# A transformer block on one core: seven-product pairs in the feed-forward stage, its operand normed first, the p product moved

## The chip, the cores and the metric

The kernel runs on one core of a Trainium2 chip. The metric is the device time of one execution in microseconds (us). The kernel before took 1504.08 us, the median of three runs from 1503.74 to 1504.20 us. The profile is one further execution, which took 1504.06 us. Its recorded span, from the first instruction to the last, is 1502.4 us, so 1.7 us lie around the span.

## The reference, cut to what matters

```
x: 256 tokens x 2048 (fp32); p: 256 x 256; w_in: 2048 x 10240; w_ffn_in: 2048 x 11264; w_ffn_out: 5632 x 2048
h   = rmsnorm(x, g_mix);  q, k, v (two mixers of 8 heads) and two gates = h @ w_in
x  += (sigmoid(g_sb) * (y_sb @ w_sb_out) + sigmoid(g_ca) * (y_ca @ w_ca_out)) @ w_mix_out     # "mix"
h   = rmsnorm(x, g_ffn);  g_ff, u_ff = split(h @ w_ffn_in, 2)
x  += (silu(g_ff) * u_ff) @ w_ffn_out                                                         # "FFN"
x  += sigmoid(rmsnorm(x, g_ple) @ w_ple_gate) * (p @ w_ple_in)                                # gate, p product
out = rmsnorm(x, g_final)
```

All data are fp32. The 256 tokens are two tiles of 128 (`t` = 0, 1); the 2048 columns of x are sixteen k tiles of 128 (`kt`).

## The kernel before, in words

**Products.** A product of fp32 matrices is made from rounded parts. Each operand is split into `hi` (rounded to the type fp32r) and `lo` (the rest, rounded too), and three TensorE matmuls are summed in PSUM: hi·hi, hi·lo, lo·hi (`row_products`, L178 to L183). The activations are the stationary operand: tables `T1`, `T2`, `T3` hold x, h or the like transposed, as 16 k tiles x (hi, lo) x 256 tokens. The weights move, 512 columns at a time.

**Pieces.** A group is one block of 512 weight columns for both token tiles. `group` (L126) cuts it into pieces of two k tiles (128x1024 numbers, 512 KB). A piece is loaded by SP into one of five `raw` buffers (L144), split by ScalarE (`hi`, L173) and VectorE (`lo`, L174) into one of three `hi` and three `lo` buffers, and used by 12 matmuls (2 k tiles x 2 token tiles x 3). `flush` (L223) writes the pieces out in order; `prefetch` (L208) keeps the loads five pieces and the splits two pieces ahead. After each piece one entry of the list `tasks` is written out, and `later` (L217) puts three empty entries ahead of its own. When a split needs a part of a table that isn't written, tasks are run until it is.

**Order on the engines.** The text order is only a priority: when the program is built, a scheduler sets the order of instructions on each engine by its own estimate of when each is ready. On the chip each engine keeps its order, and waits are semaphores.

**Tables.** `into_table` (L242) transposes four 128-column blocks of both token tiles on TensorE into PSUM (8 transposes), ScalarE copies or scales them to `hi` (L250, L256) and VectorE makes `lo` (L251, L257).

**Stages.** (1) Start: x is transposed into T1, the first v group runs, then the p product (`w_ple_in`, 4 groups of one piece, stored to memory by `pin_post`). (2) The rest of `w_in` with both attentions. (3) The out projections and the mix product; `residual_post` (L600) adds each mix block to x, sums its squares, and three pieces later puts the un-normed x into T3 with the gain `g_ffn`. (4) FFN in three blocks of 16, 16 and 12 k tiles of the hidden dimension: for each 512 hidden columns a gate group and an up group of `w_ffn_in` (8 pieces each); `g_post` and `u_post` (L630, L640) apply the token factor `rstd_ffn` and the SwiGLU, and the result goes into T2 or T1. Then four groups of `w_ffn_out` add to x. (5) The `w_ple_gate` groups and the output.

Of the kernel before, what the change touches and what calls it, by code (L numbers as in the profile page):

```python
# [35 lines left out]
LOAD_AHEAD = 5  # L36
SPLIT_AHEAD = 2
# [3 lines left out]
def block_kernel(ctx: ExitStack, tc: tile.TileContext, x, p, w_in, w_sb_out, w_ca_out, w_mix_out,  # L41
                 rel_bias, g_mix, g_ffn, g_ple, g_final, w_ffn_in, w_ffn_out, w_ple_in, w_ple_gate,
                 out):

# [20 lines left out]
    def aux(name):  # L65
        return ps_ax[-1][0].tile([P, ps_ax[-1][1]], F32, tag="ax", name=name)
# [7 lines left out]
    const("fill", [P, 832])  # L74
# [20 lines left out]
    def square_sum(n, t, c, pool):  # L95

        jk = pool.tile([P, NB], F32, tag="jk", name="jk", bufs=1)
        nc.scalar.activation(jk, x_[:, t, c * NB : (c + 1) * NB], AF.Square, accum_out=sums[n][:, t, c : c + 1])  # L98
# [27 lines left out]
    def group(kind, wsrc, n0, kts, lhs, post, needs=lambda kt: None, row0=0, keep=None):  # L126
# [4 lines left out]
        for j in range(0, len(kts), nk):  # L131
            part = kts[j : j + nk]
            r = (row0 + j) * P
            pieces.append(dict(
                g=g, kts=part, ncol=ncol, first=j == 0, last=j + nk >= len(kts),
                src=wsrc[r : r + len(part) * P, n0 : n0 + ncol].rearrange("(k p) n -> p k n", p=P),
                needs=[k for k in (needs(kt) for kt in part) if k is not None],
            ))

# [3 lines left out]

    def load(pc):  # L144
        raw = wp.tile([P, 1024], F32, tag="raw", name="raw", bufs=5)
        pc["raw"] = raw
        n = len(pc["kts"]) * pc["ncol"]
        dst = raw[:, :n].rearrange("p (k n) -> p k n", n=pc["ncol"])
        at = state["loaded"]
        if at == 0:  # L150
            for k in range(2):
                if k:
                    load_x(k, 1)
                dma_w.dma_start(dst[:, k, :], pc["src"][:, k, :])
            return
        if at < KD // 2:
            load_x(2 * at, 2)
        dma_w.dma_start(dst, pc["src"])

    def split(pc):  # L160
# [11 lines left out]
        for c in range(0, n, m):  # L172
            nc.scalar.copy(hi[:, c : c + m], raw[:, c : c + m])  # L173
            nc.vector.tensor_tensor(lo[:, c : c + m], raw[:, c : c + m], hi.bitcast(F32)[:, c : c + m], ALU.subtract)  # L174
# [3 lines left out]
    def row_products(ps, lhs, kt, t, hi, lo, a, z):  # L178
        xh = lhs[:, kt, 0, t * P : (t + 1) * P]
        xl = lhs[:, kt, 1, t * P : (t + 1) * P]  # L180
# [3 lines left out]

    def products(pc):
        g = pc["g"]
        if pc["first"]:
            g["ps"] = [ps_mm.tile([P, 512], F32, tag="mm", name=f"mm{t}") for t in range(2)]
# [12 lines left out]
        del pc["hi"], pc["lo"]  # L201
# [4 lines left out]
    state = dict(loaded=0, split=0, at=0)  # L206
# [35 lines left out]
    def into_table(dst, c, src, gain=None, key=None):  # L242

        ps = aux("tp").rearrange("p (k s) -> p k s", k=4)
        for k in range(4):
            for t in range(NT):
                nc.tensor.transpose(ps[:, k, t * P : (t + 1) * P], src[:, t, k * P : (k + 1) * P], ident)  # L247
        ks = slice(4 * c, 4 * c + 4)
        if gain is None:
            nc.scalar.copy(dst[:, ks, 0, :], ps)  # L250
            nc.vector.tensor_tensor(dst[:, ks, 1, :], ps, dst.bitcast(F32)[:, ks, 0, :], ALU.subtract)  # L251
        else:
            for k in range(4):
# [20 lines left out]
    pT = sp.tile([P, 2, 2, S], F32R, tag="pT", name="pT")  # L274
# [52 lines left out]
    tasks.append(("p", p_transposes))  # L327
# [13 lines left out]
    def pin_post(c):  # L341
        def post(ps):
            if c == 0:
                while "v" not in done:
                    run_task()
            st = sp.tile([P, NT, NB], F32, tag="pst", name="pst", bufs=2)
            for t in range(NT):
                nc.scalar.copy(st[:, t, :], ps[t])
            dma_x.dma_start(pin_d[:, :, c * NB : (c + 1) * NB], st)
        return post  # L350
# [11 lines left out]
    ps_ax.append((ctx.enter_context(tc.tile_pool(name="ps_ax", bufs=2, space=PSUM)), 1024))  # L362


    att = ExitStack()
    ap = att.enter_context(tc.tile_pool(name="att", bufs=2))
# [231 lines left out]
    late = {}  # L598

    def residual_post(c, key, gain):  # L600

        def post(ps):
# [3 lines left out]
            if key is not None:  # L606
                for t in range(NT):
                    square_sum(key, t, c, late["pool"])
                if c == 3:
                    norm(key)  # L610
                dst = T1 if key == "ple" else late["T3"]
                later(lambda: into_table(dst, c, x_[:, :, cs], gain, key))
        return post

    for c in range(4):
        group("row", w_mix_out[0], c * NB, range(KD), T1, residual_post(c, "ffn", 16), needs=lambda kt: ("mg", kt))
# [7 lines left out]
    gf = lp.tile([P, D], F32, tag="gf", name="gf")  # L624
    dma_x.dma_start(gf, g_final.rearrange("(o d) -> o d", o=1).to_broadcast((P, D)))
    flush()

    hold = {}

    def g_post(j):  # L630
        def post(ps):
            sg = lp.tile([P, NT, NB], F32, tag="sg", name="sg")
            tg = hold[j] = lp.tile([P, NT, NB], F32, tag="tg", name="tg")
# [136 lines left out]
```

## Time and profile before

| | |
|---|---|
| median of three runs | 1504.08 us |
| profiled execution | 1504.06 us |
| its span | 1502.4 us |
| TensorE matmuls busy | 1488.2 us (99%) |
| VectorE busy | 851.3 us (57%) |
| ScalarE busy | 700.8 us (47%) |
| DMA, mean over the span | 192 GB/s |

Busy time is the sum of what an engine's records cover; share is of the span. Records of neighbouring matmuls overlap, so the time that a matmul costs is read from start to start, not from its duration. A line such as L174 is the line of the kernel that issued the instruction. Idle time of an engine is put down to what it waited for.

### The profile page before, as it was taken

To read this page: it belongs to the slowest core of one execution; us is meant where nothing else is said; L and a number is where in the kernel's file an instruction comes from. 1 tells how busy PE (TensorE), PEld (TensorE's weight loads), DVE (VectorE), ACT (ScalarE), POOL (GpSimd) and SP (SyncE) were. 2 spreads that over 40 slices of the span, in tenths; PEclk is the share of its full clock that TensorE was granted. 3 is DMA by queue.
4 is the path that set the end of the run, shared out by engine and by line. 5 is a ranking of instruction groups with operands and counts; after the bars stand their busy time and mean duration, and the time that the engine had idled before them with its cause. 6 is when DMAs were issued, how large, how long until landed. Compare 5 with 4: busy or idle time off the path is not lost.

```text
span 1502.4 us, 18130 instructions
## 1 busy us (share of the span) xinstructions
PE 1488.2 (99%) x7024; PEld 1243.8 (83%) x7024; DVE 851.3 (57%) x936; ACT 700.8 (47%) x831; POOL 24.1 (2%) x45
## 2 busy tenths in 40 slices
PE   8999999999999999999999999999999999999997
PEld 6888888888888888888888888888888888888886
DVE  6566666665444565555554555455455455556576
ACT  6555554556444434554444433444443344445443
POOL 1200000000000000000000000000000000000000
PEclk9999999999999999999999999999999999999999
DMA  7865555565666666666666666666666666666573
GB/s 270 299 202 169 173 177 177 180 177 174 191 196 192 188 182 220 185 185 193 184 185 193 194 186 195 195 185 193 184 193 191 191 195 189 203 204 184 183 222 119
DMA packets 164807, 289.06 MB, mean 192 GB/s; under 512 B 9040, under 2 KB 44160, under 8 KB 164464
## 3 DMA queue, kind: packets, MB, share of 16 engines
q1 hardware_dynamic: 162560, 278.96, 61.4%
q0 software_dynamic: 2160, 8.93, 1.8%
q8 instruction: 55, 0.90, 0.2%
q14 instruction: 32, 0.26, 0.1%
HBM read 282.09 MB, written 5.77 MB: 192 GB/s over the span
## 4 chain that ended last, share of the span: by engine, by line
PE 98%; issue 1%; DMA 0%; DVE 0%; SPq 0%; POOL 0%; POOLq 0%; ACT 0%; DVEq 0%
PE mm L183 28%; PE mm L181 28%; PE mm L182 28%; PE mm L198 8%; PE mm L200 4%; PE tp L247 1%; DMA x<-in_x 0%; PE xps L286 0%; PE yp L443 0%; PE wt L534 0%; PE zp L434 0%; PE zp L433 0%; PE zp L432 0%; PE yp L434 0%; PE yp L432 0%
## 5 line engine op out<-in xcount | busy, mean ns | idle before, releaser
L174 DVE TENSOR_TENSOR lo<-raw,hi 128x1024 fp32r<-128x1024 f32 (+1 forms) x517 | 632.4, 1224 | 593.3 <-ACT hi L173 592.3
L173 ACT CAST hi<-raw 128x1024 fp32r<-128x1024 f32 (+1 forms) x517 | 543.1, 1051 | 685.3 <-PE mm L183 592.5
L182 PE MATMUL mm<-lo,T 128*128 128x512 f32 x1792 | 700.4, 391 | 0.0
L183 PE MATMUL mm<-hi,T 128*128 128x512 f32 x1792 | 697.6, 390 | 0.0
L181 PE MATMUL mm<-hi,T 128*128 128x512 f32 x1792 | 640.2, 392 | 0.0
L183 PEld LDWEIGHTS mm<-hi,T 128*128 128x128 f32 x1792 | 336.7, 188 | 69.4
L182 PEld LDWEIGHTS mm<-lo,T 128*128 128x128 f32 x1792 | 337.0, 188 | 68.6
L181 PEld LDWEIGHTS mm<-hi,T 128*128 128x128 f32 x1792 | 336.7, 188 | 68.8
L198 PE MATMUL mm<-T,hi 128*128 128x512 f32 x512 | 180.3, 398 | 0.0
L200 PE MATMUL mm<-T,lo 128*128 128x256 f32 x512 | 140.8, 280 | 0.0
L198 PEld LDWEIGHTS mm<-T,hi 128*128 128x128 f32 x512 | 95.3, 188 | 21.5
L200 PEld LDWEIGHTS mm<-T,lo 128*128 128x128 f32 x512 | 96.3, 189 | 1.2
L237 ACT COPY tm<-mm 128x256 f32<-128x256 f32 x32 | 11.9, 373 | 24.2 <-PE mm L200 24.2
L605 DVE TENSOR_TENSOR x<-mm,x 128x512 f32<-128x512 f32 x32 | 20.5, 682 | 0.0
L636 ACT ACTIVATE sg<-mm,rstd_ffn 128x512 f32<-128x512 f32 x22 | 15.0, 690 | 10.9 <-PE mm L183 10.9
L256 ACT ACTIVATE T<-tp,gT 128x256 fp32r<-128x256 f32 x32 | 15.0, 468 | 10.5 <-DVE T L257 10.5
L239 DVE TENSOR_TENSOR sm<-mm,tm 128x256 f32<-128x256 f32 x32 | 13.5, 421 | 10.4 <-ACT tm L237 10.4
L637 DVE SCALAR_TENSOR_TENSOR tg<-mm,rstd_ffn,sg 128x512 f32<-128x512 f32 x22 | 15.7, 751 | 5.0 <-ACT sg L636 5.0
L251 DVE TENSOR_TENSOR T<-tp,T 128x1024 fp32r<-128x1024 f32 x15 | 18.3, 1220 | 0.3
L257 DVE SCALAR_TENSOR_TENSOR T<-tp,gT,T 128x256 fp32r<-128x256 f32 x32 | 15.4, 480 | 4.3 <-ACT T L256 4.3
L98 ACT ACTIVATE jk<-x 128x512 f32<-128x512 f32 x24 | 15.1, 628 | 2.1 <-DMA x<-in_x 1.7
L250 ACT CAST T<-tp 128x1024 fp32r<-128x1024 f32 x15 | 15.2, 1013 | 1.1 <-PE tp L247 1.1
(166 smaller groups left out, 537.5 us busy)
## 6 DMA issues: line engine op xcount, KB each, us to landing
raw<-in_w_ffn_in SPq DMA_DIRECT2D x176, 512.0 KB, 3.7
raw<-in_w_in SPq DMA_DIRECT2D x159, 512.0 KB, 3.6
raw<-in_w_ffn_out SPq DMA_DIRECT2D x88, 512.0 KB, 4.6
raw<-in_w_mix_out SPq DMA_DIRECT2D x32, 512.0 KB, 4.0
raw<-in_w_ple_gate SPq DMA_DIRECT2D x32, 512.0 KB, 4.4
raw<-in_w_sb_out SPq DMA_DIRECT2D x16, 512.0 KB, 4.6
raw<-in_w_ca_out SPq DMA_DIRECT2D x16, 512.0 KB, 4.5
raw<-in_w_ple_in SPq DMA_DIRECT2D x4, 512.0 KB, 4.9
```

What stands on the lines that cost most here:

```text
L173: nc.scalar.copy(hi[:, c : c + m], raw[:, c : c + m])
L174: nc.vector.tensor_tensor(lo[:, c : c + m], raw[:, c : c + m], hi.bitcast(F32)[:, c : c + m], ALU.subtract)
L181: nc.tensor.matmul(ps, xh, hi, start=a, stop=False)
L182: nc.tensor.matmul(ps, xh, lo, start=False, stop=False)
L183: nc.tensor.matmul(ps, xl, hi, start=False, stop=z)
L198: nc.tensor.matmul(ps, hi[:, i, f], lhs[:, kt, :, :].rearrange("p c s -> p (c s)"), start=a, stop=False)
L200: nc.tensor.matmul(ps[:, :S], lo[:, i, f], lhs[:, kt, 0, :], start=False, stop=z)
L250: nc.scalar.copy(dst[:, ks, 0, :], ps)
L251: nc.vector.tensor_tensor(dst[:, ks, 1, :], ps, dst.bitcast(F32)[:, ks, 0, :], ALU.subtract)
L257: nc.vector.scalar_tensor_tensor(dst[:, kt, 1, :], ps[:, k, :], g, dst.bitcast(F32)[:, kt, 0, :], ALU.mult, ALU.subtract)
L605: nc.vector.tensor_tensor(x_[:, t, cs], ps[t], x_[:, t, cs], ALU.add)
L637: nc.vector.scalar_tensor_tensor(tg[:, t, :], ps[t], r, sg[:, t, :], ALU.mult, ALU.mult)
```

## The change

FFN products are no longer made group by group but in units of two column groups: for the first product the gate block and the up block of the same 512 hidden columns, for the second product two neighbouring blocks of 512 output columns. There are 11 units of the first kind and 6 of the second. A unit has 8 pairs of k tiles (6 in the second product of the last block). Pairs 2 and 4 are made by a form of Strassen's scheme with seven products instead of eight; the operands' 2x2 blocks are two token tiles by two k tiles, and two k tiles by two column groups. Each of the seven is made from three matmuls of 512 columns as before.

For such a pair the weights need three sums more (t2, t3, t4, made by VectorE and split like the others into `xh` and `xl`, which lie in a free table), and the activations need four sums (`forms`, made in `into_table`, kept in `F_in` and `F_out`). Four of the seven products go to PSUM banks of their own (`sums`), which `mid` adds up in SBUF (`C`) after pair 4; the unit's ends add `C` to the ordinary sums. PSUM is now two pools of four banks that alternate between the units.

T3 now holds the normed operand: after the last mix block, when `rstd_ffn` is known, `normal_table` scales x by it and writes the table, four tasks in all. The p product no longer runs at the start but after the mix, behind the same tasks. From the mix on there is a fourth pair of hi and lo buffers (`buffers`), and the splits may run further ahead (`prefetch`). Other edits only share buffers anew.

```diff
+PAIRS = (2, 4)
+RAW = 5
+    def unit(wsrc, n0s, kts, lhs, forms, ext, mid, post, needs, row0=0):
+        state["unit"] = state.get("unit", -1) + 1
+        pool, side = late["ps"][:: 1 if state["unit"] % 2 == 0 else -1]
...
+            if i in PAIRS:
+                pieces.append(dict(pc, src=src, pair=True, first=i == PAIRS[0], last=i == PAIRS[-1]))
+            else:
+                for b in range(2):
+                    pieces.append(dict(pc, src=[src[b]], block=b, first=i == 0, last=2 * i + 2 == len(kts)))
...
+    def split_pair(pc, raw1, raw2):
...
+        xl, xh = room[:, :1536], room[:, 1536:]
+        xf = late["pool"].tile([P, 1536], F32, tag="xf", name="xf")
...
+        (h1, l1), (h2, l2) = buffers(1024), buffers(1024)
+        nc.scalar.copy(h1, raw1)
+        minus(t3, b[1][:, 1, :], b[1][:, 0, :])
+        minus(b[1][:, 0, :], b[1][:, 0, :], b[0][:, 0, :])
+        nc.scalar.copy(h2, raw2)
+        minus(t2, b[1][:, 1, :], b[1][:, 0, :])
+        minus(t4, b[0][:, 1, :], t2)
+        nc.scalar.copy(xh, xf)
+        minus(l1, raw1, h1.bitcast(F32))
+        minus(l2, raw2, h2.bitcast(F32))
+        minus(xl, xf, xh.bitcast(F32))
...
+    def pair_products(pc):
...
+        if a:
+            while tasks:
+                run_task()
+            g["sums"] = [g["side"].tile([P, 512], F32, tag="mm", name=f"su{i}") for i in range(4)]
...
+        for ps, x, w, own in ((q1, (kt, 0), 0, True), (c11, (kt2, 0), 1, False), (c12, 3, 3, False), (q5, 0, 2, True),
+                              (q6, 1, 4, True), (q7, 2, 5, True), (c21, (kt2, 1), 6, False)):
+            three(ps, *stationary(x), hi[w], lo[w], a and own, z and own)
+        if z:
+            g["mid"](g)
...
     def prefetch():
-        while state["loaded"] < min(len(pieces), state["at"] + LOAD_AHEAD + 1):
+        while state["loaded"] < len(pieces) and state["raw"] + len(pieces[state["loaded"]]["src"]) <= RAW:
...
-        ahead = 1 if state["at"] < KD // 2 else SPLIT_AHEAD
-        while state["split"] < min(len(pieces), state["at"] + ahead + 1):
-            split(pieces[state["split"]])
+        room = 2 if state["at"] < KD // 2 else 4 if "pool" in late else 3
+        while state["split"] < state["loaded"] and state["split"] <= state["at"] + 3:
+            pc = pieces[state["split"]]
+            if state["split"] > state["at"] and sum(map(size, pieces[state["at"] : state["split"] + 1])) > room:
+                break
+            split(pc)
...
+    def into_table(dst, c, src, gain=None, key=None, forms=None, pool=None):
...
+            if forms is not None and kt // 2 in PAIRS:
+                af = late["pool"].tile([P, 2, S], F32, tag="af", name="af", bufs=2)
...
+                nc.vector.tensor_tensor(fm[:, 0, :], a21, a22, ALU.add)
+                minus(fm[:, 2, :], a11, a21)
+                minus(fm[:, 1, :], fm[:, 0, :], a11)
+                minus(fm[:, 3, :], a12, fm[:, 1, :])
+                f = forms(kt)
+                nc.scalar.copy(f[:, 0], fm)
+                minus(f[:, 1], fm, f.bitcast(F32)[:, 0])
...
+    def normal_table(c):
+        xn = late["pool"].tile([P, NT, NB], F32, tag="sg", name="xn")
+        for t in range(NT):
+            nc.scalar.activation(xn[:, t, :], x_[:, t, c * NB : (c + 1) * NB], AF.Identity,
+                                 scale=rstd["ffn"][:, t : t + 1])
+        into_table(late["T3"], c, xn, 16, "ffn", lambda kt: late["F"][0][kt // 4 - 1])
+    def mix_post(c):
...
+            residual_done(c, "ffn")
+            if c == 3:
+                for cc in range(4):
+                    tasks.append((None, lambda cc=cc: normal_table(cc)))
...
-    for c in range(4):
-        group("row", w_ple_in[0], c * NB, range(2), pT, pin_post(c), needs=lambda kt: "p")
...
+    tasks.append(("p", p_transposes))
+    for c in range(4):
+        group("row", w_ple_in[0], c * NB, range(2), pT, pin_post(c), needs=lambda kt: "p")
+    flush()
...
+    def mid(g):
+        q1, q5, q6, q7 = g["sums"]
+        C = g["C"] = lp.tile([P, 4, NB], F32, tag="C", name="C", bufs=2)
+        nc.scalar.copy(C[:, 0, :], q1)
+        for i, q, j in ((2, q6, 0), (1, q7, 2), (3, q5, 1), (2, q5, 2)):
+            nc.vector.tensor_tensor(C[:, i, :], q, C[:, j, :], ALU.add)
+    def in_post(dst, c, key):
+        def post(g, b):
+            C = g["C"]
+            for t in range(NT):
+                i = 2 * b + t
+                nc.vector.tensor_tensor(C[:, i, :], g["ps"][i], C[:, i, :], ALU.add)
+            if b == 0:
+                sg = lp.tile([P, NT, NB], F32, tag="sg", name="sg")
+                for t in range(NT):
+                    nc.scalar.activation(sg[:, t, :], C[:, t, :], AF.Sigmoid)
+                for t in range(NT):
+                    nc.vector.tensor_tensor(C[:, t, :], C[:, t, :], sg[:, t, :], ALU.mult)
+            else:
+                for t in range(NT):
+                    nc.vector.tensor_tensor(C[:, t, :], C[:, t, :], C[:, 2 + t, :], ALU.mult)
+                later(lambda: into_table(dst, c, C[:, :2, :], key=key, pool=g["pool"],
+                                         forms=lambda kt: late["F"][1][kt // 4 - 1]))
...
+        for c in (0, 2):
+            unit(w_ffn_out[0], (c * NB, (c + 1) * NB), range(nk), T2, lambda kt: late["F"][1][kt // 4 - 1],
+                 T3 if last else T1, mid, out_unit_post(c, last), lambda kt, key=key: (key, kt), row0=k0)
```

`out_unit_post` adds the PSUM block to `C` and `C` to x (two VectorE instructions for each token tile); in the last block it also sums squares and puts x into T1 for the gate.

## Rows read from the trace of the kernel before

**Rows 1.** Page: busy us, share of the span, instructions, by engine.

```profile
PE 1488.2 (99%) x7024; PEld 1243.8 (83%) x7024; DVE 851.3 (57%) x936; ACT 700.8 (47%) x831; POOL 24.1 (2%) x45
```

**Rows 2.** Page: the chain that ended last, share by engine.

```profile
PE 98%; issue 1%; DMA 0%; DVE 0%; SPq 0%; POOL 0%; POOLq 0%; ACT 0%; DVEq 0%
```

**Rows 3.** Stretches: us, busy by engine (instructions), granted clock, DMA share, GB/s.

```profile
0.00:60.00 60.00, 54.71 (x261) 44.70 (x262) 34.89 (x53) 36.45 (x59) 9.57 (x21) 1.00 0.81 273
...
671.40:1404.30 732.90, 732.90 (x3290) 606.72 (x3289) 387.17 (x361) 313.72 (x329) 2.23 (x3) 1.00 0.64 191
```

**Rows 4.** Timeline of TensorE, mix stage: start us, us, instruction; starts of pieces, transposes.

```profile
649.10 0.62 PE L181 MATMUL mm<-hi,T 128*128 128x512 f32 x2
...
651.82 0.62 PE L181 MATMUL mm<-hi,T 128*128 128x512 f32 x2
...
654.54 0.62 PE L181 MATMUL mm<-hi,T 128*128 128x512 f32 x2
655.00 0.60 PE L247 MATMUL tp<-ident,x 128*128 128x128 f32 x4
...
657.75 0.60 PE L247 MATMUL tp<-ident,x 128*128 128x128 f32 x4
```

**Rows 5.** Groups by shape: count, busy us, mean ns, idle before it.

```profile
L174 DVE TENSOR_TENSOR lo<-raw,hi 128x1024 fp32r<-128x1024 f32 x515 | 631.0, 1226 | 592.5 <-ACT hi L173 591.4
L173 ACT CAST hi<-raw 128x1024 fp32r<-128x1024 f32 x515 | 541.9, 1053 | 684.6 <-PE mm L183 592.5 <-PE mm L198 52.6 <-issue 29.8
...
L605 DVE TENSOR_TENSOR x<-mm,x 128x512 f32<-128x512 f32 x32 | 20.5, 682 | 0.0
```

**Rows 6.** Timeline of VectorE: a dense stretch of attention, then the tail.

```profile
264.25 1.23 DVE L174 TENSOR_TENSOR lo<-raw,hi 128x1024 fp32r<-128x1024 f32 x1 [2.57 <-ACT hi L173]
265.39 0.42 DVE L427 TENSOR_TENSOR sl<-qT,sh 128x256 fp32r<-128x256 f32 x1
265.73 0.69 DVE L427 TENSOR_TENSOR sl<-kT,sh 128x512 fp32r<-128x512 f32 x1
266.33 0.69 DVE L410 TENSOR_TENSOR T<-yp,T 128x512 fp32r<-128x512 f32 x1
...
1482.82 0.69 DVE L683 TENSOR_TENSOR sgr<-sgr,pi 128x512 f32<-128x512 f32 x1 [1.51 <-ACT sgr L682]
1483.54 0.69 DVE L684 TENSOR_TENSOR x<-x,sgr 128x512 f32<-128x512 f32 x1
```

**Rows 7.** Timeline of ScalarE and VectorE: one split, waiting for a free buffer.

```profile
601.08 1.05 ACT L173 CAST hi<-raw 128x1024 fp32r<-128x1024 f32 x1 [1.67 <-PE mm L183]
602.17 1.23 DVE L174 TENSOR_TENSOR lo<-raw,hi 128x1024 fp32r<-128x1024 f32 x1 [1.49 <-ACT hi L173]
```

**Rows 8.** Timeline of three engines: last mix block to the norm.

```profile
671.59 1.28 DVE L605 TENSOR_TENSOR x<-mm,x 128x512 f32<-128x512 f32 x2
674.71 0.17 DVE L104 TENSOR_SCALAR ms_ffn<-ms_ffn 128x2 f32<-128x2 f32 x1
674.96 0.73 POOL L105 TENSOR_TENSOR rstd_ffn<-ms_ffn,mhalf 128x2 f32<-128x2 f32 x1 [85.89 <-DVE ms_ffn L104]
```

**Rows 9.** Timeline of ScalarE: small table steps, and stores of the p product.

```profile
681.65 0.47 ACT L256 ACTIVATE T<-tp,gT 128x256 fp32r<-128x256 f32 x1
...
48.01 1.08 ACT L348 COPY pst<-mm 128x512 f32<-128x512 f32 x2 [2.40 <-DMA pin_d<-pst]
```

**Rows 10.** Timeline of TensorE: first matmuls after the idle start, then later ones.

```profile
7.83 0.63 PE L183 MATMUL mm<-hi,T 128*128 128x512 f32 x1
8.26 0.63 PE L182 MATMUL mm<-lo,T 128*128 128x512 f32 x1
...
11.99 0.40 PE L182 MATMUL mm<-lo,T 128*128 128x512 f32 x1
12.22 0.39 PE L183 MATMUL mm<-hi,T 128*128 128x512 f32 x1
```

**Rows 11.** Page, DMA issues: queue, count, KB each, us to landing.

```profile
raw<-in_w_ffn_in SPq DMA_DIRECT2D x176, 512.0 KB, 3.7
```

More of the change, by code (lines that the diff above doesn't have):

```diff
@@ L95, in square_sum @@
     def square_sum(n, t, c, pool):
[L97 removed]
+        jk = pool.tile([P, NB], F32, name="jk", **(dict(tag="af", bufs=2) if pool is late.get("pool") else dict(tag="jk", bufs=1)))
         nc.scalar.activation(jk, x_[:, t, c * NB : (c + 1) * NB], AF.Square, accum_out=sums[n][:, t, c : c + 1])
@@ L142, in load_x, with load_piece, buffers, minus @@
         dma_w.dma_start(x_[:, :, cs], xr[:, :, cs])
+    def load_piece(src, ncol):
+        raw = wp.tile([P, 1024], F32, tag="raw", name="raw", bufs=RAW)
+        n = src.shape[1] * ncol
+        return raw[:, :n], raw[:, :n].rearrange("p (k n) -> p k n", n=ncol)
     def load(pc):
[L145 to L148, printed above, removed]
         at = state["loaded"]
[L150 to L158, printed above, removed]
+        pc["raw"] = []
+        for src in pc["src"]:
+            raw, dst = load_piece(src, pc["ncol"])
+            pc["raw"].append(raw)
+            state["raw"] += 1
+            if at == 0:
+                for k in range(2):
+                    if k:
+                        load_x(k, 1)
+                    dma_w.dma_start(dst[:, k, :], src[:, k, :])
+                continue
+            if at < KD // 2:
+                load_x(2 * at, 2)
+            dma_w.dma_start(dst, src)
+    def buffers(n):
+        state["hl"] += 1
+        i = state["hl"]
+        out = []
+        for tag in ("hi", "lo"):
+            if "pool" in late and i % 4 == 0:
+                t = late["pool"].tile([P, 1024], F32R, tag=tag, name=tag)
+            else:
+                t = wp.tile([P, 1024], F32R, tag=tag, name=tag, bufs=3)
+            out.append(t[:, :n])
+        return out
+    def minus(out, a, b):
+        nc.vector.tensor_tensor(out, a, b, ALU.subtract)
     def split(pc):
@@ L163, in split @@
                 run_task()
-        n = len(pc["kts"]) * pc["ncol"]
-        raw = pc.pop("raw")[:, :n]
+        raws = pc.pop("raw")
+        state["raw"] -= len(raws)
+        if pc["g"]["kind"] == "unit" and len(raws) == 2:
+            return split_pair(pc, *raws)
+        raw, = raws
+        n = raw.shape[1]
         if pc["g"]["keep"] is None:
-            hi = wp.tile([P, 1024], F32R, tag="hi", name="hi", bufs=3)[:, :n]
-            lo = wp.tile([P, 1024], F32R, tag="lo", name="lo", bufs=3)[:, :n]
+            hi, lo = buffers(n)
         else:
@@ L605, in post @@
                 nc.vector.tensor_tensor(x_[:, t, cs], ps[t], x_[:, t, cs], ALU.add)
[L606 to L612, printed above, removed]
+            residual_done(c, "ffn")
+            if c == 3:
+                for cc in range(4):
+                    tasks.append((None, lambda cc=cc: normal_table(cc)))
         return post
     for c in range(4):
-        group("row", w_mix_out[0], c * NB, range(KD), T1, residual_post(c, "ffn", 16), needs=lambda kt: ("mg", kt))
+        group("row", w_mix_out[0], c * NB, range(KD), T1, mix_post(c), needs=lambda kt: ("mg", kt))
     flush(until=("mg", KD - 1))
```

216 lines of the change are left out of this document (135 added, 81 removed).

## The prediction

> **What bounds the kernel now.** I read the page's busy times first, then the chain of waits, the stretches, and last the timelines of the places that the change touches. TensorE's matmuls cover 99% of the span, VectorE 57%, ScalarE 47% [rows 1]; the chain that ended last is 98% TensorE [rows 2]. In the FFN's stretch, 732.9 us from the last mix block to the last FFN block, TensorE is busy without a gap, VectorE for 387.2 us and ScalarE for 313.7 us [rows 3]. A piece starts every 2.72 us (649.10, 651.82, 654.54), so a matmul of 512 columns costs 2.72 / 12 = 0.2266 us, whatever its record's length; a piece with four transposes takes 657.75 - 654.54 = 3.21 us, so a transpose costs 0.12 us [rows 4]. The splits wait on the right side: `hi` for a buffer that a matmul releases, `lo` for `hi` [rows 5, 7]. From the release (601.08) a piece is split at 602.17 + 1.23 = 603.40 us, 2.3 us later, once in 2.72 us [rows 7]. So time falls if TensorE gets fewer matmuls and stays fed.
>
> **The products.** A pair of k tiles in a unit is 2 k tiles x 2 column blocks x 2 token tiles x 3 = 24 matmuls, by the new form 7 x 3 = 21. Two pairs in each of 17 units save 2 x 3 x 17 = 102 matmuls of 512 columns: 102 x 0.2266 = **23.1 us**. The transposes stay, and the p product's 48 matmuls (10.9 us) only change place. This term is all gain, since nothing else fills TensorE's path [rows 2, 4]. Weight bytes are the same.
>
> **What VectorE now has to do.** Instructions that follow each other without need start closer than they last: after a 1024 wide one the next starts 1.14 us later, after 512 wide 0.60, after 256 wide 0.34; where one needs the other's result, 0.72 for 512 wide [rows 6]. For 1536 wide (no row) I add the step from 512 to 1024: 1.14 + 0.54 = 1.68 (ends: 1.14, and 1.14 + 0.72). For 128 wide the ends are 0.17 (a two-number instruction [rows 8]) and 0.34; I take 0.28, nearer to the 256 wide one.
> A pair piece: four dependent sums 4 x 0.72, two `lo` 2 x 1.14, `xl` 1.68, together 6.8 us, for 21 x 0.2266 = 4.76 us of TensorE. Two single pieces in its place were 2.3 us.
> A unit of the first product: 12 single `lo` 13.7, two pairs 13.7, `mid` 4 x 0.72 = 2.9, the ends' eight instructions 8 x 0.66 = 5.3, the table 2 x 0.60 = 1.2: 36.8 us, and 1.7 more where forms are made (four sums and one `lo`). TensorE: 186 x 0.2266 + 8 x 0.12 = 43.1 us. A unit of the second product: 35.6 against 42.1 us. So VectorE goes from 53% of the stretch [rows 3] to 85 to 89%: still under TensorE on average.
> ScalarE: 12 `hi` at 1.05 [rows 5] are 12.6 us, two pairs (two `hi` and `xh`, by width 1.5) 7.2, the rest (one copy, two sigmoids, the table) some 3: 23 us in 43, no bound.
>
> **Where that gets tight.** With four buffers a piece's split can begin when the fourth buffer before it is free. (a) From the first end of a unit to the point in pair 2 where `xl` is used (its fifth product): one piece, four pieces, eight transposes and 12 matmuls, 2.7 + 10.9 + 1.0 + 2.7 = 17.3 us of TensorE. VectorE has to do the ends 5.3, two `lo` 2.3, the pair 6.8 and the table 1.2 to 2.9: 15.6 to 17.3 us. Margin 0 to 1.7 us. (b) From pair 2's start to the same point of pair 4: 4.8 + 5.4 + 2.7 = 12.9 us against two `lo`, a pair and one `lo` ahead, 10.3 us. Margin 2.6 us. VectorE may idle no longer than that in these stretches. Before, it idled 1.5 us ahead of each `lo`, waiting for ScalarE [rows 7]; but then it had nothing else, and now the sums can run while ScalarE rounds. I take 0.13 us of stall for each of 15 units, **+2 us**. Ends: 0, and 1.4 us for each of 17 units, which would eat the whole gain.
> The last two units have six pairs: VectorE 9.1 + 13.7 + 2.9 + 5.3 = 31.0 against 138 x 0.2266 = 31.3 us, and the second also makes two tables for the gate, 8 x 0.44 = 3.5, against 16 x 0.12 = 1.9 more. It is short by up to 1.3 us, and any wait adds. **+2 us** (0 to 6).
>
> The Trainium skill (VectorE: DVE Perf Modes, Terms) says that each VectorE operation ends with a pipeline flush before the next can issue. Here the next one's record starts 0.09 us before the last one's ends [rows 6], and I go by that. With full durations (1.226 and 0.682 [rows 5]) a unit would need about 39 us instead of 36.8; by that rule margin (a) is gone and the sum would come out some 8 us worse, which is the first rival's direction.
>
> **The FFN operand normed first.** Before, the tables were made from un-normed x, and only the last block's had to follow the mix. Now all four wait for the norm. The chain in the trace: the adds start at 671.59, the last step before the power ends at 674.88, the power runs 674.96 to 675.69 [rows 8]: 4.1 us. Then two scalings of 512 columns (1.3), four transposes (0.5), two `hi` (0.47 each [rows 9]): the first table part is there about 6.5 us after the mix ends. The p product, 10.9 us, stands behind it and needs none of it. If its first piece runs ahead of the first transposes, TensorE is covered. In text order those transposes come before it, but the built order need not be the text's: the first matmuls of both token tiles already run together (the rows of two, x2 [rows 4]), which isn't the written order.
> Behind this ScalarE is crowded: four tables (5.2 for scaling, 2 x 1.5 plain, 2 x 2.6 with forms: 13.4), eight stores of p (4.4, and in the trace 2.4 us of waiting for the store's DMA [rows 9]), and the splits up to pair 2 (7.2). That is 27.4 us from 4.1 us after the mix on, so done at 31.5. TensorE wants pair 2 at 10.9 + 10.9 + 32 x 0.12 = 25.6 us. Only the last table (2.8) can wait; if it does, pair 2 is some 3 us late, if not up to 6. **+4 us**. Ends: 0, if the splits are set into the gaps; 8.6, if TensorE keeps the text order (5.5 for the first transposes, 2.5 and 0.6 for the next ones).
>
> The clock: after the idle start the matmuls came 0.43 us apart (7.83, 8.26), the pace of 512 columns at 1.2 GHz, later 0.23 [rows 10]; the granted clock column shows 1.00 there all the same [rows 3]. The Trainium skill (TensorE: Matmul & The Clock Gate, Part 1) says that an idle TensorE falls to half its clock. Here that would speak against the change only if the gap at the norm opens; by the start's rows (about 4 us at double cost) it would add 2 us, and I put it into the upper end.
>
> **Moved at no cost.** At the start TensorE idles 60 - 54.7 = 5.3 us in the first 60 us [rows 3], p product and all; if that product covered another wait there, I can't name it, and put it under 2 us, at nothing in the sum. POOL's queue loses p's load and stores there and gets them at the mix; the power stands ahead of the stores. SP's queue carries the same 512 KB loads; one lands in 3.7 us [rows 11], and DMA is 64% busy [rows 3], so pairs that take two buffers at once are fed unless VectorE holds the five.
>
> **Sum.** Against the profiled execution, 1504.06 us (span 1502.4 and 1.7 around it; the median of the runs is the same to 0.02): 1504.06 - 23.1 + 2 + 2 + 4 = **1489.0 us**, own range 1483 to 1494.
>
> **Rivals.**
> 1. *Half is eaten in the pair stretches.* VectorE's order is fixed ahead, and waits for ScalarE of 0.7 us fall into margin (a) of each unit: 17 x 0.7 = 12 in place of the 2. 1504.06 - 23.1 + 12 + 2 + 4 = 1499 us. For it: margins of 0 to 1.7 us. Against: four buffers, and sums that need no buffer.
> 2. *All is hidden.* No stall at the norm nor in the units: 1504.06 - 23.1 = 1481 us. For it: greedy filling of gaps; against: ScalarE's 27 us.
> 3. *The norm's gap is open,* text order on TensorE, and the clock falls: 1504.06 - 23.1 + 8.6 + 2 + 4 = 1495.5 us.
> 4. *VectorE's chain is the bound: slower.* If a pair's split runs as one chain with ScalarE (sums 2.9, `xh` 1.5, `l1`, `l2` 2.5, `xl` 1.8, one 1.05 of ScalarE between: 9.7) with the three `lo` of (b) not in its gaps (3.7) and started only when pair 2 frees its first buffer (1.6 in), it needs 15.0 us for 12.9: 2.1 us, and 17 units make 36 us. 1504.06 - 23.1 + 36 + 6 = 1523 us. It decides from 1.4 us a unit on. For it: `lo` waited for `hi` in nearly all of VectorE's idle [rows 5]; against: the sums need only `raw`.
>
> **Chances.** Forecast 0.55, rival 1 0.18, rival 2 0.12, rival 3 0.05, rival 4 0.10. Range 1481 to 1500: it holds the forecast, 2, 3 and most of 1. About 0.2% (3 us) is what can be told from no change. Faster: 0.55 + 0.12 + 0.05 + 0.13 of rival 1 = 0.85; within 0.2% 0.05; slower 0.10.
>
> **What would show it.** After: 102 matmuls of 512 columns fewer; pair pieces of 4.76 us with no TensorE gap behind them; VectorE busy about 85% in FFN; p's matmuls between mix and FFN with a gap of some 4 us around the tables; stalls in the last two units. Wrong would be: gaps ahead of each pair 2 or 4 (rivals 1, 4), or `xl` as what they wait for at more than 1.4 us a unit.

## The result, and the profile after

The changed kernel took **1488.8 us**, the median of four runs (1487.35 to 1491.76), beside 1503.95 us for the kernel before (four runs, 1503.74 to 1504.20). The ratio is 0.9902, 95% interval 0.9885 to 0.9919. The profiled execution took 1487.96 us, its span 1486.2 us.

The page's busy times (busy us, share of the span, instructions), the chain that ended last, and the loads, to be laid beside [rows 1, 2, 11]:

```profile
PE 1467.7 (99%) x6922; PEld 1224.5 (82%) x6922; DVE 1071.5 (72%) x1291; ACT 764.0 (51%) x917; POOL 24.8 (2%) x45
...
PE 91%; DVE 3%; DMA 2%; ACT 1%; issue 1%; SPq 0%; POOL 0%; POOLq 0%; DVEq 0%; ACTq 0%
...
raw<-in_w_ffn_in SPq DMA_DIRECT2D x176, 512.0 KB, 4.3
raw<-in_w_ffn_out SPq DMA_DIRECT2D x88, 512.0 KB, 4.7
```

TensorE has 7024 - 6922 = 102 instructions fewer, and the chain now passes through VectorE, DMA and ScalarE for some 6% of the span. The stretches (columns as in [rows 3]) say where: the norm, the steady units, the end of the FFN.

```profile
640.00:700.00 60.00, 58.90 (x273) 48.11 (x272) 41.70 (x58) 42.18 (x65) 3.49 (x5) 1.00 0.64 202
700.00:1300.00 600.00, 600.00 (x2687) 497.10 (x2686) 505.21 (x580) 306.70 (x317) 0.00 (x0) 1.00 0.64 198
1300.00:1420.00 120.00, 116.57 (x525) 94.18 (x524) 99.54 (x132) 63.99 (x87) 3.47 (x5) 1.00 0.62 201
```

In 600 us of steady units TensorE is never without work, although VectorE is busy for 84% of them. TensorE idles around the norm and at the end.

To weigh this I add up, for each stretch, by how much the distance from one TensorE instruction's start to the next exceeds 0.2266 us (0.12 for a transpose). I call that the excess; it is worked out from the timelines, one profile for each kernel:

| excess of TensorE, us | norm, 640 to 700 | 700 to 1300 | 1300 to 1420 |
|---|---|---|---|
| before | 0.2 | 1.1 | 0.6 |
| after | 2.1 | 0.7 | 6.1 |

So 1504.06 - 23.1 + (8.9 - 1.9) = 1488.0 us, the profiled execution's own time: nothing else is left to explain in this execution. Taking the p product away from the start costs nothing there: in its first 60 us TensorE idles 5.0 us, 5.3 before [rows 3].

### The profile page after: what moved, and what is told of

Its sections match the earlier page's. It is cut to its first block, busy times and chain, and to the rows that moved or that the text cites. A ratio compares the mean times of both kernels' runs of the same rounds, so it can differ in the third digit from the quotient of the medians.

```text
span 1486.2 us, 18409 instructions
## 1 busy us (share of the span) xinstructions
PE 1467.7 (99%) x6922; PEld 1224.5 (82%) x6922; DVE 1071.5 (72%) x1291; ACT 764.0 (51%) x917; POOL 24.8 (2%) x45
## 4 chain that ended last, share of the span: by engine, by line
PE 91%; DVE 3%; DMA 2%; ACT 1%; issue 1%; SPq 0%; POOL 0%; POOLq 0%; DVEq 0%; ACTq 0%
PE mm L254 24%; PE mm L255 24%; PE mm L256 24%; PE mm L315 8%; PE mm L317 4%; PE su L255 2%; PE su L256 2%; PE su L254 2%; DVE lo L207 1%; DMA raw<-in_w_ffn_out 1%; PE tp L374 1%; DMA pin_d<-pst 1%; DVE T L207 0%; ACT hi L225 0%; DMA x<-in_x 0%
## 5 line engine op out<-in xcount | busy, mean ns | idle before, releaser
L225 ACT CAST hi<-raw 128x1024 fp32r<-128x1024 f32 (+1 forms) x449 | 471.6, 1051 | 534.9 <-PE mm L256 419.8
L255 PE MATMUL mm<-lo,T 128*128 128x512 f32 x1576 | 615.7, 391 | 0.0
L256 PE MATMUL mm<-hi,T 128*128 128x512 f32 x1576 | 614.5, 392 | 0.3 <-DVE T L402 0.3
L254 PE MATMUL mm<-hi,T 128*128 128x512 f32 x1576 | 588.0, 391 | 3.8 <-ACT hi L225 2.2
L254 PEld LDWEIGHTS mm<-hi,T 128*128 128x128 f32 x1576 | 296.0, 188 | 65.9 <-ACT hi L225 3.2
L256 PEld LDWEIGHTS mm<-hi,T 128*128 128x128 f32 x1576 | 296.2, 188 | 60.8 <-DVE T L402 0.7
L207 DVE TENSOR_TENSOR T<-xf,T 128x1536 fp32r<-128x1536 f32 x34 | 59.5, 1751 | 4.4 <-ACT T L246 4.3
L207 DVE TENSOR_TENSOR xf<-raw 128x512 f32<-128x512 f32 x68 | 46.5, 684 | 17.5 <-DMA raw<-in_w_ffn_out 8.8
L243 ACT CAST hi<-raw 128x1024 fp32r<-128x1024 f32 x34 | 35.9, 1057 | 39.1 <-PE mm L256 26.3
L246 ACT CAST T<-xf 128x1536 fp32r<-128x1536 f32 x34 | 50.4, 1482 | 10.3 <-DVE xf L207 10.2
L794 DVE TENSOR_TENSOR C<-su,C 128x512 f32<-128x512 f32 x68 | 45.3, 687 | 11.5 <-PE su L256 9.5
L240 ACT CAST hi<-raw 128x1024 fp32r<-128x1024 f32 x34 | 36.1, 1061 | 25.1 <-PE mm L256 19.5
L801 DVE TENSOR_TENSOR C<-mm,C 128x512 f32<-128x512 f32 x44 | 29.9, 682 | 0.0
L255 PE MATMUL mm<-T,T 128*128 128x512 f32 (+1 forms) x66 | 24.1, 365 | 0.1
L254 PE MATMUL mm<-T,T 128*128 128x512 f32 (+1 forms) x66 | 24.1, 365 | 0.0
```

The costliest lines, as they stand in the source:

```text
L207: nc.vector.tensor_tensor(out, a, b, ALU.subtract)
L240: nc.scalar.copy(h1, raw1)
L243: nc.scalar.copy(h2, raw2)
L246: nc.scalar.copy(xh, xf)
L254: nc.tensor.matmul(ps, xh, hi, start=a, stop=False)
L255: nc.tensor.matmul(ps, xh, lo, start=False, stop=False)
```

## The experiments

**Theory A.** The pairs save 23.1 us; the steady units cost nothing; what is given back is lost at the norm (ScalarE waits for a store of the p product) and in the last two units (VectorE has too much to do). **Rivals.** The steady units stall a little each, as predicted; or the end lacks a load buffer rather than VectorE time; or the split chain of any pair costs TensorE something. The kernel before ran beside each experiment and took 1503.99 to 1504.09 us (median). A "gap" below is one such excess.

| kernel | median us (lowest to highest) | ratio to before, 95% interval | excess: norm, middle, end |
|---|---|---|---|
| no pairs | 1503.2 (1501.86 to 1504.23) | 0.9994 (0.9985 to 1.0004) | 0.1, 0.3, 0.1 |
| sixth load buffer | 1483.52 (1482.05 to 1483.94) | 0.9863 (0.9848 to 0.9877) | 0.2, 0.8, 4.2 |
| last two units plain | 1482.33 (1481.66 to 1483.78) | 0.9855 (0.9839 to 0.9871) | 0.2, 0.7, 0.1 |
| p product at the start | 1494.81 (1493.77 to 1495.53) | 0.9939 (0.9924 to 0.9954) | 9.8, 0.7, 6.1 |
| p stores without a wait | 1487.59 (1486.35 to 1488.79) | 0.9890 (0.9875 to 0.9904) | 0.2, 0.7, 9.9 |
| last sums on GpSimd | 1485.24 (1484.94 to 1485.56) | 0.9874 (0.9859 to 0.9889) | 0.4, 0.7, 5.1 |
| 4 sums more in a unit | 1486.74 (1486.33 to 1488.17) | 0.9887 (0.9871 to 0.9904) | 0.2, 0.7, 7.6 |
| 8 sums more in a unit | 1498.43 (1496.66 to 1500.62) | 0.9963 (0.9951 to 0.9976) | 0.2, 8.9, 9.9 |
| one pair in the last two units | 1482.08 (1481.19 to 1484.10) | 0.9856 (0.9841 to 0.9871) | 0.2, 0.7, 0.3 |
| sixth buffer and GpSimd | 1482.51 (1481.57 to 1483.56) | 0.9857 (0.9843 to 0.9872) | 0.2, 0.8, 2.7 |
| three edits together | 1480.72 (1480.30 to 1482.27) | 0.9846 (0.9831 to 0.9860) | 0.2, 0.8, 0.2 |

**1. No pairs.** Units, normed operand and moved p product stay; all pairs are made from ordinary products.

```diff
-            if i in PAIRS:
+            if i in pairs:          # pairs=() for every unit
```

> All edits but the seven-product pairs: every pair of k tiles is two single pieces again, so no sums, forms, mid; the units, the norm first, p behind the mix and the fourth buffer stay. Theory (the gain is 102 matmuls x 0.2266 = 23.1 us and nothing else): the time comes back to that of before plus the 2 us lost at the norm, 1506 us (1504.5 to 1507.5), with no stall in the last two units, and the stretch of the FFN units as long per matmul as before. Rival (part of the gain comes from the other edits, the fourth buffer or the wider units): under 1503 us.

Measured 1503.2 us, the same as before within what can be told, and under the expected range: the 2 us at the norm didn't come, its excess is 0.1 us. The rest of the change brings nothing and costs nothing. The pairs bring 1503.2 - 1488.8 = 14.4 us. That is 23.1 less about 8.7, and neither stall shows without the pairs.

**2. What the steady units can bear.** Four, then eight useless 512 wide sums on VectorE, written at the first end of each of 15 units; their result isn't used.

```diff
+                for _ in range(4):        # 8 in the other kernel
+                    nc.vector.tensor_tensor(junk, C[:, 2, :], C[:, 3, :], ALU.add)
```

> The change with four more VectorE sums of 512 columns (2.4 us, into a scratch tile) at the first end of each of the 15 units before the last two. The prediction's margin (a), 0 to 1.7 us there, says that 0.7 to 2.4 us a unit reach TensorE: 10 to 36 us, 1499 to 1525 us. Rival (the backlog is spread over the whole unit, since splits run up to four buffers ahead; VectorE was busy 543.7 of 650 us in the middle, so 7 us in a unit of 43 are free): under 3 us in all, 1488 to 1491 us.

> Eight useless 512 wide sums on VectorE at the first end of each of the 15 units ahead of the last two, 4.8 us a unit; their result is not used. Theory A (a unit stalls when VectorE's whole work exceeds TensorE's time for it, not at single stretches): VectorE's need is 36.8 to 38.5 plus 4.8, so 41.6 to 43.3 us against 43.1 and 42.1 us of TensorE: about at the limit, TensorE's excess between 700 and 1300 us 2 to 15 us, time 1490 to 1502. Rival B (the margin of 0 to 1.7 us between a unit's end and pair 2 decides, as I had predicted): 3 us or more for each of 15 units, time over 1530. Rival C (VectorE still has room): no excess, time within 2 us of 1488.8.

The middle stretch with four, then with eight (columns as above):

```profile
700.00:1300.00 600.00, 600.00 (x2688) 496.93 (x2687) 539.15 (x636) 305.98 (x316) 0.00 (x0) 1.00 0.62 198
```
```profile
700.00:1300.00 600.00, 595.98 (x2652) 490.56 (x2651) 557.74 (x679) 295.41 (x309) 0.00 (x0) 1.00 0.60 194
```

With VectorE busy for 90% (539.15 of 600) TensorE doesn't wait at all; at 93% it does. That is what a whole unit bears, and not what margin (a) of the prediction bears, because the sums run elsewhere than they are written. With four, all 60 of them run between `mid` and the first end (L801 below), where VectorE idles 5.1 to 5.4 us in each of these units of the changed kernel, and 2.7 to 2.9 here:

```profile
1001.12 0.69 DVE L804 TENSOR_TENSOR junk<-C 128x512 f32<-128x512 f32 x1
...
1002.86 1.41 DVE L804 TENSOR_TENSOR junk<-C 128x512 f32<-128x512 f32 x2
...
1005.32 0.68 DVE L804 TENSOR_TENSOR junk<-C 128x512 f32<-128x512 f32 x1
...
1010.47 0.68 DVE L801 TENSOR_TENSOR C<-mm,C 128x512 f32<-128x512 f32 x1
```

With eight, five to seven run there, and one to three behind the first end. So a unit bears 2.4 us more on VectorE (four sums at 0.60), and not every unit bears 4.8; margin (a) by itself isn't tested. With eight sums the total came out as expected, but not in the way of either theory: 7.2 of the 8.9 us lie between 815 and 875 us, at the end of one unit and the start of the next, and the other units hold. The largest gap there, on TensorE (start us, us, instruction, what it waited for):

```profile
863.28 0.40 PE L253 MATMUL mm<-hi,T 128*128 128x512 f32 x1
866.70 0.50 PE L253 MATMUL mm<-hi,T 128*128 128x512 f32 x1 [3.02 <-ACT hi L224]
...
867.31 0.63 PE L255 MATMUL mm<-hi,T 128*128 128x512 f32 x1
867.74 0.63 PE L254 MATMUL mm<-lo,T 128*128 128x512 f32 x1
```

There VectorE had stood 2.26 us for a load (until 846.81), and its `xl` (the last rounded part of a pair, see the prediction) ended 0.06 us before TensorE took it at 862.71. Why that unit and not the others isn't settled.

**3. The last two units plain, or with one pair.** The first makes them from ordinary products (12 matmuls more, 2.7 us), the second leaves pair 2 only (6 more, 1.4 us).

```diff
+OUT_PAIRS = lambda last: () if last else PAIRS      # (2,) if last: the second kernel
```

> The last two units (second product of the last block) without pairs; the other 15 as changed. 12 matmuls more, 2.7 us. Theory A and B (the pairs' work on VectorE makes the gaps there, through buffers or directly): the 4.8 us go, about 1 us of the gate's first pieces too, so 1488.8 + 2.7 - 5.5 = 1486 us (1485 to 1487.5). Rival C (the gaps come from the end of FFN itself: residual adds, tables, the gate's loads): the gaps stay and 1491 us result.

> Only the last two units change: one pair instead of two, everything else as in the changed kernel. 6 matmuls more (1.36 us). Theory A (VectorE has more work in these two units than TensorE gives it time; one pair fewer is 3 us less work per unit): the gaps of TensorE after 1300 us fall from 6.1 us to under 1, time 1483 to 1485 (with the wait at the norm between 0 and 2 us). Rival B (what lacks there is the raw buffer, not the work): 2 to 4 us of gaps stay, time 1486 to 1488.

Both came out under what was expected. Without pairs the end's excess is 0.1 us and the time 1482.33 us, where 1485 to 1487.5 had been expected; that sum still held the norm's 2 us, which its profile doesn't have. One pair fewer in each removes the gaps too: TensorE's excess at the end falls from 6.1 to 0.3 us, and the time to 1482.08 us. Of the 6.7 us gained, 6.1 - 0.3 - 1.4 = 4.4 are the end; the other 2 are the norm, where this profile has 0.2 us instead of 2.1 (see 6). From 1350 to 1375 us, the changed kernel and then the one with one pair:

```profile
1350.00:1375.00 25.00, 22.32 (x101) 16.85 (x100) 23.80 (x35) 13.49 (x24) 1.45 (x2) 1.00 0.59 189
```
```profile
1350.00:1375.00 25.00, 25.00 (x120) 20.89 (x119) 22.03 (x29) 16.14 (x25) 2.01 (x3) 1.00 0.72 234
```

VectorE has 22.0 us to do in these 25, not 23.8, while TensorE does more.

**4. A sixth load buffer, and the last sums on GpSimd.** One edit gives the loads room, one takes eight 512 wide sums off VectorE in the last two units; then both, with both pairs kept.

```diff
-        raw = wp.tile([P, 1024], F32, tag="raw", name="raw", bufs=RAW)
+        if "pool" in late and state["rawn"] % 6 == 0:
+            raw = late["pool"].tile([P, 1024], F32, tag="rawx", name="raw", bufs=1)
...
-                nc.vector.tensor_tensor(x_[:, t, cs], x_[:, t, cs], C[:, i, :], ALU.add)
+                (nc.gpsimd if last else nc.vector).tensor_tensor(x_[:, t, cs], x_[:, t, cs], C[:, i, :], ALU.add)
```

> The change with a sixth raw buffer from the late part on (a 5 KB filler and a small constant are moved to make room). Theory A (in the last two units VectorE holds the raw buffers too long, the loads then go out in a burst and land 9 us later): the 4.8 us of TensorE gaps between 1350 and 1400 us fall under 2 us, 1485 to 1486.5 us. Theory B (VectorE has too much work there, whatever the buffers): the gaps stay within 1 us of 4.8, 1488 to 1489 us.

> The change, but in the last two units the eight sums of x and C run on GpSimd in place of VectorE, 8 x 0.6 = 4.8 us of VectorE's work gone, pairs and buffers as they were. Theory B (VectorE's amount of work in the last two units is the bound; a sixth raw buffer left 4.1 of the 6.1 us of gaps there, a small part): the gaps there fall from 6.1 us to 1 to 3 us and the time to 1484 to 1486 us, if GpSimd's own sums (perhaps twice as long) do not hold up the gate's tables. Theory A (buffers): 1488 to 1489 us.

> Both pairs stay in the last two units, with a sixth load buffer and with the 8 last sums of those units on GpSimd. Theory A (amount of VectorE's work and room to load early both count, each taking a part): gaps of TensorE after 1300 us 1 to 3 us where the sixth buffer alone left 4.15 and GpSimd alone 5.07; time 1480.5 to 1482.5. Rival B (the two take the same part away): gaps stay at 4 us, time 1483 to 1484. Rival C (all gaps go): time 1479 to 1480, under the kernel with one pair there.

The end's excess goes from 6.1 to 4.2, 5.1 and with both 2.7 us: gains of 1.9 and 1.0, and of 3.4 together, a little more than their sum. GpSimd alone had been expected to leave 1 to 3 us; its sums took 1.3 to 2.3 us each, and two of the gaps that are left (0.6 and 0.3 us) wait for them. The sixth buffer's time, 1483.52 us, lies under both expectations, and GpSimd's 1485.24 in its range, because their profiles lack most of the norm's excess too (0.2 and 0.4 us). VectorE is still full there, 24.94 of 25 us, in the kernel with both:

```profile
1350.00:1375.00 25.00, 23.54 (x109) 18.59 (x108) 24.94 (x30) 16.38 (x26) 8.00 (x6) 1.00 0.65 205
```

So the buffer rival is right for a third at most. That the pairs make the gaps is shown by experiment 3. That they do it by their work on VectorE is argued: from a VectorE without idle time, and from the gain when GpSimd takes sums over. A pair also wants two loads at once, and no run here parts the two.

**5. The p product back at the start.**

```diff
+    for c in range(4):
+        group("row", w_ple_in[0], c * NB, range(2), pT, pin_post(c), needs=lambda kt: "p")     # in the start stage
```

> The change with the p product back at the start; between mix and FFN nothing then stands behind the norm. Theory (p's 10.9 us cover the norm's chain of about 6.5 us): TensorE stands still some 5 to 6.5 us at the norm in place of 1.4, ScalarE is free of p's stores, and the time is 1492 to 1494 us; if the idle time also lowers the clock, the next matmuls come 0.43 us apart for a while and it is up to 1496. Rival (ScalarE's queue is the bound there and p covers nothing): 1486 to 1489 us.

Measured 1494.81 us, 6.0 more, as expected for the case that the clock falls. TensorE, from its last mix matmul on, and then two stretches behind it (columns as above, the granted clock third from the right):

```profile
668.76 0.39 PE L256 MATMUL mm<-hi,T 128*128 128x512 f32 x1
675.87 2.15 PE L374 MATMUL tp<-ident,xn 128*128 128x128 f32 x8 [6.72 <-ACT xn L754]
...
678.54 0.63 PE L255 MATMUL mm<-lo,T 128*128 128x512 f32 x1
678.97 0.63 PE L254 MATMUL mm<-hi,T 128*128 128x512 f32 x1
```
```profile
677.60:681.00 3.40, 3.40 (x10) 2.52 (x9) 1.81 (x4) 2.72 (x6) 0.00 (x0) 0.50 0.00 0
681.00:690.00 9.00, 9.00 (x48) 7.51 (x48) 5.41 (x11) 6.76 (x11) 0.00 (x0) 1.00 0.04 9
```

Without the p product TensorE stands for 6.9 us while the norm's chain runs, and its clock then is 1.2 GHz (0.50) until about 681, with 0.43 us a matmul. The moved p product covers that chain.

**6. The p stores without a wait.** The two staging tiles hold two stores each, so no copy waits for a store.

```diff
+            if c % 2 == 0:
+                late["pst"] = lp.tile([P, 4, NB], F32, tag="C", name="pst", bufs=2)
+            st = late["pst"][:, NT * (c % 2) : NT * (c % 2) + NT]
```

> The change with the four p stores packed into both halves of two buffers, so that no store's copy waits for an earlier store to land. Theory (the gap at the norm, 1.4 us in the profile of the change and near nothing in three of the runs since, is ScalarE standing in front of a store that has not landed, and its length varies with that landing): no wait of the p copies for a store, TensorE's gaps between 640 and 700 us under 0.3 us, the median 1 to 2 us under that of the change, 1487 us, and less spread. Rival (ScalarE's crowd of table steps and splits, not the store): the gap stays at 1 us or more.

The norm's excess is gone (0.2 us), as expected, but the end's grew to 9.9 in its profile: a gap of 3.27 us, and then a granted clock of 0.50:

```profile
1372.50:1378.60 6.10, 5.85 (x14) 4.60 (x15) 5.47 (x6) 5.09 (x6) 0.00 (x0) 0.50 0.45 135
1378.60:1390.00 11.40, 11.40 (x51) 9.39 (x50) 6.26 (x7) 3.17 (x3) 0.56 (x1) 0.99 0.73 246
```

So the median is only 1.2 us lower, inside the spread of both. Eight other kernels here keep the staging as it was, with the p product behind the mix; in their profiles the copies waited 0 to 1.3 us for a store where the changed kernel's profile has 2.9, and their norm has 0.1 to 0.4 us of excess. The second store, which the last wait is for, landed after 7.5 us in the changed kernel's profile and after 4.9 to 5.9 in those eight. So the norm's cost hangs on when a store lands, and varies.

**7. Together.** Sixth buffer, p stores without a wait, one pair in each of the last two units.

> The sixth raw buffer, the packed p stores, and one pair in place of two in the last two units (6 matmuls, 1.4 us, more than the change). If the gaps there come from VectorE's amount of work, one pair (6.8 - 2.3 = 4.5 us less for each unit) leaves under 0.5 us: 1504.0 - 96 x 0.2266 = 1482.2, 1481.5 to 1482.7 us, which would equal or beat the version without pairs there (1482.3). If one pair still stalls by over 1 us: 1483 to 1484 us.

1480.72 us: 8.1 us below the changed kernel and 23.4 below the one before. Up to 1375 us, and behind it, the end of the FFN has no gap:

```profile
1350.00:1375.00 25.00, 25.00 (x121) 20.86 (x120) 21.24 (x27) 15.11 (x27) 2.01 (x3) 1.00 0.75 241
```

By the count of matmuls it should be 1504.06 - 23.1 + 1.4 = 1482.3. The 1.6 us below that can be placed in its profile: the three stretches have 1.2 us of excess beside 1.9 before, and TensorE idles 4.1 us in the first 60 us, 5.3 before [rows 3]. That idle time at the start is 4.0 to 5.7 us in the profiles here, so its part is no gain of these edits.

## Why the prediction was right

The forecast was 1489.0 us, and its sum of given-back time was 2 + 2 + 4 = 8 us; measured are 7.0. The total is right, but its three terms are not: they came out at -0.4, 5.5 and 1.9 us. That their errors cancel, and to 0.2 us, is luck.

**The products.** Right: 102 matmuls, 23.1 us, all gain.

**VectorE's work.** Right in size: 84% of the steady units, where I had 85 to 89. The groups of its instructions after (columns as in [rows 5]):

```profile
L207 DVE TENSOR_TENSOR lo<-raw,hi 128x1024 fp32r<-128x1024 f32 x515 | 627.8, 1222 | 326.6 <-ACT hi L225 324.7
L207 DVE TENSOR_TENSOR T<-xf,T 128x1536 fp32r<-128x1536 f32 x34 | 59.5, 1751 | 4.4 <-ACT T L246 4.3
L207 DVE TENSOR_TENSOR xf<-raw 128x512 f32<-128x512 f32 x68 | 46.5, 684 | 17.5 <-DMA raw<-in_w_ffn_out 8.8 <-DMA raw<-in_w_ffn_in 8.4
```

Idle ahead of `lo` fell from 592.5 [rows 5] to 326.6 us. In one steady unit of the first product, on VectorE:

```profile
1001.38 2.81 DVE L794 TENSOR_TENSOR C<-su,C 128x512 f32<-128x512 f32 x4 [0.59 <-PE su L256]
...
1013.58 0.68 DVE L801 TENSOR_TENSOR C<-mm,C 128x512 f32<-128x512 f32 x1
1015.44 0.69 DVE L207 TENSOR_TENSOR xf<-raw 128x512 f32<-128x512 f32 x1 [1.17 <-DMA raw<-in_w_ffn_in]
...
1026.60 1.75 DVE L207 TENSOR_TENSOR T<-xf,T 128x1536 fp32r<-128x1536 f32 x1
1028.26 1.22 DVE L207 TENSOR_TENSOR lo<-raw,hi 128x1024 fp32r<-128x1024 f32 x1
...
1031.74 0.28 DVE L389 TENSOR_TENSOR fm<-af 128x128 f32<-128x128 f32 x1
1031.94 0.28 DVE L207 TENSOR_TENSOR fm<-af 128x128 f32<-128x128 f32 x1
...
1040.63 3.48 DVE L207 TENSOR_TENSOR lo<-raw,hi 128x1024 fp32r<-128x1024 f32 x3
1044.47 2.81 DVE L794 TENSOR_TENSOR C<-su,C 128x512 f32<-128x512 f32 x4 [0.36 <-PE su L256]
```

From `mid` to `mid` it is 43.09 us, the 43.1 that I had worked out for TensorE. The 1536 wide step takes 1.66 to the next start (I took 1.68), the 128 wide one 0.20 (I took 0.28).

**The stall of the steady units: +2 predicted, none measured.** This is the mis-sized term with the wrong reason. VectorE does run without a pause here, from 1015.44 to 1044.11, as margin (a) feared. But I had taken each pair's 21 matmuls as one block in written order. TensorE, just behind that `xl` step:

```profile
1031.12 0.39 PE L254 MATMUL mm<-T,T 128*128 128x512 f32 x1
1031.35 0.39 PE L254 MATMUL mm<-hi,T 128*128 128x512 f32 x1
1031.58 0.39 PE L255 MATMUL mm<-T,T 128*128 128x512 f32 x1
...
1034.52 0.39 PE L254 MATMUL su<-T 128*128 128x512 f32 x1
...
1035.20 0.39 PE L254 MATMUL mm<-hi,T 128*128 128x512 f32 x1
```

The built order lays matmuls of single pieces between the pair's, and VectorE makes the next table (`T<-tp`) only behind the pair. `xl` is ready at 1028.35, its first use is at 1031.58: 3.2 us of margin where I had 0 to 1.7. From the first end (1013.58) VectorE needs 14.8 us to the end of `xl`, where I had 15.6 to 17.3 with the table in it, and TensorE needs 18.0 us to its use, where I had 17.3. Over the 30 pairs of the units ahead of the last two this margin is 2.3 to 4.8 us. With four sums more it is 2.6 to 4.8, since they run in other idle time (experiment 2); with eight it falls to 0.06 at the gap shown there. So the reason why nothing stalled is read from the built order; no run changed margin (a) alone.

The Trainium skill (VectorE: DVE Perf Modes, Terms) says that each VectorE operation ends with a pipeline flush before the next issues; the rows above have the next record start 0.09 us before the last one ends (1028.35 and 1028.26), as [rows 6] did, so the rival direction drawn from that rule fell too.

**The last two units: +2 predicted, +5.5 measured.** Right in that VectorE is short there, in size short by 3.5. I had VectorE short by up to 1.3 us (0.9 with the 0.39 us from start to start of the gate's table steps after, where I had 0.44) and let "any wait adds" stand without a price. The chain of waits shows the price (start us, us, step); then two loads that GpSimd issues beside it, and ScalarE and TensorE behind it:

```profile
1363.53 1.15 DVE lo L207
1364.69 8.88 DMA raw<-in_w_ffn_out
```
```profile
1364.08 1.45 POOL L854 DMA_DIRECT2D pi<-pin_d  x2 [689.01 <-DVE x L823]
```
```profile
1372.17 0.39 PE L256 MATMUL su<-hi,F 128*128 128x512 f32 x1
1373.66 1.04 ACT L225 CAST hi<-raw 128x1024 fp32r<-128x1024 f32 x1 [3.23 <-DMA raw<-in_w_ffn_out]
1374.76 0.50 PE L254 MATMUL mm<-hi,T 128*128 128x512 f32 x1 [2.20 <-ACT hi L225]
```

VectorE is late with a `lo`, so a load buffer comes free late, so a load starts late, and it takes 8.9 us where the median is 4.7. A late VectorE costs here not its own lag but a load behind it, 2.4 us in one gap. The sixth buffer takes a part of just that away. The load isn't slow by VectorE's doing alone: two 512 KB loads of the stored p product (`pi`) are under way with it and land after 7.57 and 8.95 us. With one pair the loads beside `pi` took 7.5 to 8.3 us too, but started earlier, and TensorE didn't wait. No run moves the loads of `pi` alone. The other gaps are short: some 1.6 us between 1353 and 1367, most of it waits for `lo` and `xl`, and 1.3 near 1400, at the gate's tables.

**The norm: +4 predicted, +1.9 measured.** The p product did run ahead (`mm<-hi,pT` from 658.14), and the chain that I priced at 6.5 us (its terms add up to 6.8) was covered. (The first transposes started 8.5 us after the adds, 666.31 - 657.85, where I had 5.5.) What was late is a copy that waited for a p store. I had counted such a wait, 2.4 us [rows 9], in ScalarE's work, but not as one of TensorE's:

```profile
657.85 1.28 DVE L737 TENSOR_TENSOR x<-mm,x 128x512 f32<-128x512 f32 x2
658.14 0.39 PE L254 MATMUL mm<-hi,pT 128*128 128x512 f32 x1
661.12 0.73 POOL L115 TENSOR_TENSOR rstd_ffn<-ms_ffn,mhalf 128x2 f32<-128x2 f32 x1 [83.08 <-DVE ms_ffn L114]
662.49 1.34 ACT L729 ACTIVATE xn<-x,rstd_ffn 128x512 f32<-128x512 f32 x2
666.31 1.03 PE L374 MATMUL tp<-ident,xn 128*128 128x128 f32 x8
...
672.65 0.58 ACT L779 COPY pst<-mm 128x512 f32<-128x512 f32 x1 [1.93 <-DMA pin_d<-pst]
673.29 0.50 PE L254 MATMUL mm<-hi,T 128*128 128x512 f32 x1 [0.96 <-ACT pst L779]
```

ScalarE's 27.4 us of work there did not make pair 2 late: the splits were set into the gaps, my lower end. So the step that failed here is the overlap, pair 2 behind ScalarE.

**The rivals.** Rival 2 (all hidden, 1481) was nearest to the truth of the steady units and of the norm; with one pair less at the end the time comes within 1.1 us of it. Rival 3 is experiment 5 in kind: an open norm with the clock's fall cost 6 us on top. Rivals 1 and 4 fell: no gap lies ahead of a pair in the steady units.

**Left open.** The changed kernel's runs spread over 4.4 us, those of before over 0.5. The end's gap, which in two profiles of other kernels was followed by a low clock, the p store and the start (4.0 to 5.7 us of idle time) are likely sources, but only one of the four runs has a profile.

## What to carry to other kernels

Count the work of an engine that becomes nearly full over a whole unit and in the built order, not over one stretch of the written order: at 90% busy VectorE still cost nothing here. Look for the price where a stage is shorter than the steady one, since a late engine there also holds load buffers and turns its lag into a late load. See in the trace where a useless instruction really runs before reading its price. When a form with more work elsewhere pays everywhere but in the last units, use it less there: one pair fewer cost 1.4 us and removed 5.8.

## What the hardware showed beyond the forecast

- After a gap TensorE can come back at half its clock (1.2 GHz): granted 0.50 behind 3.27 us (experiment 6), 0.43 us from start to start behind 3.19 us (experiment 2, eight sums) and behind 2.50 us (four sums), where a gap of 2.36 us in the changed kernel was followed by the usual 0.23. But a gap of 2.95 us in the kernel with eight more sums was too, so in these rows the length of the gap alone doesn't tell. The Trainium skill (TensorE: Matmul & The Clock Gate, Part 1) says that an idle TensorE falls to half its clock; experiment 5 agrees, with 0.50 granted behind 6.9 us.
- Beside other loads (260 GB/s from 1364 to 1374, 198 in the steady units) a 512 KB load took 8.9 us; the median of the `w_ffn_out` loads is 4.7 and that of `w_ffn_in` before 3.7 [rows 11].
